# Expert stage in another order: the next expert's features and first products between this expert's steps, and the second 64 slots in one of two arms

## The chip, the cores and the metric

The kernel runs on one core of one Trainium2 chip. The metric is the device time of one execution in microseconds; the profile of one execution stands beside it. The engines are TensorE (PE), VectorE (DVE), ScalarE (ACT), GpSimd (POOL) and SyncE (SP, which only issues transfers here).

## What is computed

The kernel is a model of several stages, of which one appears twice here: a mixture of experts, after the mixing stage of each of two layers. Cut to what matters, the reference is:

```python
def hier_moe(h, w_rg, b_rg, w_re, b_re, w_gate, w_up, w_down):
    ...                                   # softmax scores, two experts of 32 for each token
    order = jnp.argsort(flat_e)           # token slots sorted by expert
    ...
    x_buf = h_pad[buf_tok].reshape(nblk, MOE_BLOCK, d)

    def run_block(args):
        xb, e = args
        return (jax.nn.silu(xb @ w_gate[e]) * (xb @ w_up[e])) @ w_down[e]

    y = lax.map(run_block, (x_buf, blk_e)).reshape(total, d)
    return jnp.zeros((n, d), h.dtype).at[tok_sorted].add(y[dest] * w_sorted[:, None].astype(h.dtype))
```

All is float32. A token has 1024 features; an expert has 512 hidden ones, so its gate, up and down matrices are 2 MB each.

## The kernel before

`moe` (L1035) runs the stage, once in each layer. Slots are dealt out so that each of the 32 experts (`NE`) has one block of 128 slots; tokens beyond that go to overflow blocks, which a loop at the end of `moe` runs with `expert`, one block a turn. The loop over the 32 experts in `experts` is unrolled. A block's 128 slots are two halves of 64. The first half always runs. The second runs only where the expert has more than 64 slots: `more` is read from the index table `tix` on every engine (L1286), and `tc.If(more < T)` (L1287) is a branch that each engine takes for itself.

For one expert the loop does the following.

- POOL gathers the rows of the expert after next into one of three buffers `xg` (`ex_load`, L1198).
- SP issues the next expert's weights: twelve tiles `wr` of 512 KB, four each of gate, up and down (`ex_load_w`, `wraw` at L105). They go through a ring of 32 tiles; a load into a tile waits until the products that read it are over. A down tile is 128 rows of 4 KB that lie 16 KB apart, one for each partition.
- `ex_in` (L1228): 16 first products on PE, eight slices of 128 features by gate and up. Gate goes to partitions 0 to 63 of one PSUM tile `ea`, up to the others. The profile counts each as two passes, 32 in all.
- `ex_act`: silu on ScalarE (L1234), then the product with the up half on VectorE (L1235), which writes `sg`.
- `ex_x` of the next expert: eight transposes of 64 rows of `xg` on PE (L1218), copied by VectorE to `xT` (L1220).
- `past[e]()`, in the experts 0 to 3: small steps that spread the gains, count the overflow and write its lists.
- `ex_at`: four transposes of `sg` on PE (L1241), copied by VectorE to `aT` (L1243).
- `ex_out` (L1252): eight second products (16 passes) into another PSUM tile `ea`; ScalarE scales them by the slot's weight in layer 0 (L1255), VectorE by weight and gain in layer 1 (L1257); POOL scatters `ey` to `Y` in DRAM (L1258).
- then the branch, and in its arm `ex_half`: the whole chain again for the other 64 slots, each step behind the one before.

PSUM tiles come from one pool of eight banks with the tag `b`; `xT`, `sg`, `aT` and `ey` have two buffers each. The order on each engine is set by a scheduler that places instructions as they become ready, within the order of the code on either side of a branch; `keep_in_program_order` pins an instruction against others that are pinned.

Of the kernel before, what the change touches and what calls it, by code (L numbers as in the profile page):

```python
# [8 lines left out]
F32 = mybir.dt.float32  # L9
# [4 lines left out]
AF = mybir.ActivationFunctionType  # L14
ALU = mybir.AluOpType
# [4 lines left out]
P = 128  # L20
# [5 lines left out]
NE = 32  # L26
# [16 lines left out]
class Ker:  # L43
# [1156 lines left out]

    def ex_w(self, name, l, e):
        w = self.I[name]
        w = w[l, e] if isinstance(e, int) else w[l, bass.ds(e, 1)].rearrange("o a b -> (o a) b")
        return w.rearrange("(p k) f -> p k f", p=P)

    def ex_load_w(self, l, e):

        gu = [self.ex_w(n, l, e) for n in ("moe_w_gate", "moe_w_up")]
        d = self.ex_w("moe_w_down", l, e)
        gu = [[self.wraw(w[:, k:k + 2, :]) for w in gu] for k in (0, 2, 4, 6)]  # L1210
        return gu, [self.wraw(d[:, k:k + 1, :]) for k in range(4)]

    def ex_x(self, xg, h, px, ps):

        r = slice(h * 64, h * 64 + 64)
        pt = ps.tile([P, 512], F32, name="pt", tag="b")
        for k in range(8):
            self.nc.tensor.transpose(pt[:, k * 64:k * 64 + 64], xg[r, k * P:(k + 1) * P], self.ident[r, r])  # L1218
        x = px.tile([P, 8, 64], F32, name="xT", tag="xT")
        self.nc.vector.tensor_copy(x, pt.rearrange("p (k t) -> p k t", k=8))  # L1220
        return x

    def ex_in(self, w, x, ps):

        a = ps.tile([P, 512], F32, name="ea", tag="b")
        for k in range(8):
            for j in range(2):
                self.nc.tensor.matmul(a[j * 64:j * 64 + 64, :], x[:, k, :], w[0][k // 2][j][:, k % 2, :], start=k == 0, stop=k == 7)  # L1228
        return a
# [8 lines left out]
    def ex_at(self, sg, px, ps):  # L1238
        pt = ps.tile([P, 512], F32, name="pt", tag="b")
        for k in range(4):  # L1240
            self.nc.tensor.transpose(pt[:, k * 64:k * 64 + 64], sg[64:, k * P:(k + 1) * P], self.ident[64:, 64:])  # L1241
        at = px.tile([P, 4, 64], F32, name="aT", tag="aT")
        self.nc.vector.tensor_copy(at, pt[:, :256].rearrange("p (k t) -> p k t", k=4))  # L1243
        return at

    def ex_out(self, w, at, idx, wl, Y, T, px, ps):

        nc = self.nc
        acc = ps.tile([P, 512], F32, name="ea", tag="b")
        for k in range(4):  # L1250
            for c in range(2):
                nc.tensor.matmul(acc[c * 64:c * 64 + 64, :], at[:, k, :], w[1][k][:, 0, c * 512:c * 512 + 512], start=k == 0, stop=k == 3)  # L1252
        y = px.tile([P, 512], F32, name="ey", tag="ey")
        if self.gain is None:
            nc.scalar.mul(y, acc, wl)  # L1255
        else:
            nc.vector.scalar_tensor_tensor(y, acc, wl, self.gain, ALU.mult, ALU.mult)  # L1257
        nc.gpsimd.indirect_dma_start(Y.rearrange("t (h d) -> (t h) d", h=2), bass.IndirectOffsetOnAxis(ap=idx, axis=0), y, None,  # L1258
                                     bounds_check=4 * T - 1, oob_is_err=False)

    def ex_half(self, w, h, xg, idx, wl, Y, T, px, ps):

        a = self.ex_in(w, self.ex_x(xg, h, px, ps), ps)
        self.ex_out(w, self.ex_at(self.ex_act(a, px), px, ps), idx[:, h], wl[:, h], Y, T, px, ps)

    def experts(self, l, tix, idx, wl, xg, hD, Y, T, px, ps, past, gains):

        nc = self.nc
        for e in range(2):
            self.ex_load(tix[:, e:e + 1], xg[e % 3], hD, T)  # L1270
        x = self.ex_x(xg[0], 0, px, ps)
        w = [self.ex_load_w(l, 0)]
        for e in range(NE):
            if e + 2 <= NE:
                self.ex_load(tix[:, e + 2:e + 3], xg[(e + 2) % 3], hD, T)
            if e + 1 < NE:
                w.append(self.ex_load_w(l, e + 1))
# [12 lines left out]
            if e == NE - 1:  # L1290
                gains()

    def expert(self, l, e, idx, wl, xg, Y, T, px, ps):
        w = self.ex_load_w(l, e)
        for h in range(2):
            self.ex_half(w, h, xg, idx, wl, Y, T, px, ps)


    def rpb_tables(self, pool):
# [865 lines left out]
```

## Time and profile before

| | us |
|---|---|
| three executions | 3675.94, 3684.01, 3686.07 |
| their median | 3684.01 |
| the profiled execution | 3679.17 |
| its span, first to last instruction | 3677.4 |
| PE busy | 3303.7 (90% of the span) |
| PE weight loads busy | 2146.6 (58%) |
| VectorE busy | 1483.9 (40%) |
| ScalarE busy | 1037.0 (28%) |
| GpSimd busy | 499.2 (14%) |

The profiled execution is one of its own, not one of the three. Busy times are a sum over stages with different limits, so a share of 90% doesn't say that PE sets the end of each stage; and a PE that is busy may run at either of two clock levels. `PEclk` in a row is the mean clock that was granted in its stretch, as a share of full speed (0.95 over the whole execution). In a row of the timeline, what stands in brackets is how long the engine was idle before the instruction and what it had waited for; `PEq`, `PEldq` or `SPq` is the sequencer of an engine, which handles branches, loads of registers and issues of transfers.

### The profile page before, as it was taken

How to read it: one execution, taken by the hardware profiler on the slowest of the kernel's cores; microseconds unless marked ns; L12 is line 12 of the kernel's file. 1: busy time of each engine (PE TensorE's matmuls, PEld its weight loads, DVE VectorE, ACT ScalarE, POOL GpSimd, SP SyncE). 2: the span in 40 equal slices, each digit the busy share in tenths (PEclk: the TensorE clock that was granted, in tenths of full speed). 3: DMA queues.
4: the chain of work that ended last, by engine and by line, in shares of the span. 5: the costliest groups of instructions: out<-in, count | busy, mean ns of one | idle time of the engine just before them, and what ended most of it. 6: DMA issues, size and time to landing. Idle time of an engine off the chain costs nothing.

```text
span 3677.4 us, 44411 instructions
## 1 busy us (share of the span) xinstructions
PE 3303.7 (90%) x16560; PEld 2146.6 (58%) x16560; DVE 1483.9 (40%) x2766; ACT 1037.0 (28%) x1809; POOL 499.2 (14%) x581
## 2 busy tenths in 40 slices
PE   7999988888888879998888887798999999999998
PEld 5954565332223378776333232676888877778887
DVE  3475664111111166666211111536543447355343
ACT  3465541111101134443000000325332324333232
POOL 1053511110011023331111110303000000000000
PEclk9999999898989889999999999899999999999999
DMA  5134456985799542226899995522323324233331
GB/s 197 49 132 150 150 182 241 384 344 191 273 362 393 211 143 78 66 60 237 328 407 394 398 396 203 187 81 73 112 93 97 92 44 101 81 93 103 92 92 46
DMA packets 351067, 676.15 MB, mean 184 GB/s; under 512 B 43028, under 2 KB 194772, under 8 KB 349408
## 3 DMA queue, kind: packets, MB, share of 16 engines
q1 hardware_dynamic: 313816, 626.50, 48.1%
q0 software_dynamic: 17584, 25.94, 2.0%
q10 hardware_dynamic: 19416, 20.34, 1.8%
q8 instruction: 160, 2.62, 0.3%
q14 instruction: 91, 0.75, 0.1%
HBM read 676.74 MB, written 29.45 MB: 192 GB/s over the span
## 4 chain that ended last, share of the span: by engine, by line
PE 34%; issue 10%; DMA 4%; DVE 2%; ACT 1%; POOL 0%; SPq 0%; POOLq 0%; ACTq 0%; DVEq 0%
PE aw L197 6%; PE aw L198 6%; PE aw L199 6%; PE acc L197 5%; PE acc L199 5%; PE acc L198 5%; DMA Y<-ey,idx 4%; PE s L1989 1%; PE o L1995 0%; ACT wh L116 0%; PE o L495 0%; PE pt L1725 0%; PE pt L299 0%; DMA yp<-Y 0%; DVE xO L1573 0%
## 5 line engine op out<-in xcount | busy, mean ns | idle before, releaser
L1228 PE MATMUL ea<-wr,xT 128*64 128x512 f32 x2368 | 544.0, 599 | 27.9 <-PEq L1287 13.6
L117 DVE TENSOR_TENSOR wh<-wr,wh 128x1024 fp32r<-128x1024 f32 (+2 forms) x276 | 339.2, 1235 | 319.5 <-ACT wh L116 319.0
L197 PE MATMUL aw<-hh,wh 128*128 128x512 f32 (+1 forms) x1216 | 446.7, 368 | 3.7 <-ACT wh L116 2.6
L198 PE MATMUL aw<-hl,wh 128*128 128x512 f32 (+1 forms) x1216 | 447.2, 368 | 1.6 <-DVE hl L193 1.6
L199 PE MATMUL aw<-hh,wh 128*128 128x512 f32 (+1 forms) x1216 | 446.0, 367 | 0.0
L116 ACT CAST wh<-wr 128x1024 fp32r<-128x1024 f32 (+2 forms) x276 | 281.0, 1026 | 448.8 <-PE acc L199 292.5
L1252 PE MATMUL ea<-wr,aT 128*64 128x512 f32 x1184 | 368.4, 780 | 42.2 <-DVE aT L1243 26.5
L1228 PEld LDWEIGHTS ea<-wr,xT 128*64 128x64 f32 x2368 | 190.3, 137 | 360.0 <-issue 272.8
L1220 DVE COPY xT<-pt 128x512 f32<-128x512 f32 x74 | 51.1, 691 | 660.0 <-PE pt L1218 660.0
L1234 ACT ACTIVATE sg<-ea 64x512 f32<-64x512 f32 x74 | 76.4, 1032 | 808.5 <-PE ea L1228 808.5
L197 PEld LDWEIGHTS aw<-hh,wh 128*128 128x128 f32 x1216 | 230.9, 190 | 45.6 <-ACT wh L116 3.5
L198 PEld LDWEIGHTS aw<-hl,wh 128*128 128x128 f32 x1216 | 231.0, 190 | 44.9 <-issue 3.5
L199 PEld LDWEIGHTS aw<-hh,wh 128*128 128x128 f32 x1216 | 230.8, 190 | 43.0 <-issue 3.5
L1252 PEld LDWEIGHTS ea<-wr,aT 128*64 128x64 f32 x1184 | 107.5, 175 | 245.5 <-issue 190.4
L467 POOL TENSOR_TENSOR pp<-pp,rc 128x768 f32<-128x768 f32 (+3 forms) x192 | 211.5, 1109 | 258.4 <-DVE rc L466 248.2
L1258 POOL DMA_INDIRECT Y<-ey,idx x74 | 74.8, 1011 | 961.8 <-DVEq L1287 355.0
L465 ACT ACTIVATE pp<-s,nm 128x768 f32<-128x768 f32 (+3 forms) x192 | 137.1, 716 | 156.6 <-DVE nm L1470 78.3
L197 PE MATMUL acc<-wh,hh 128*128 128x512 f32 (+2 forms) x480 | 177.4, 370 | 0.0
L198 PE MATMUL acc<-wh,hh 128*128 128x512 f32 (+2 forms) x480 | 176.3, 367 | 0.0
L199 PE MATMUL acc<-wh,hl 128*128 128x512 f32 (+2 forms) x480 | 175.9, 366 | 0.0
L1241 PE MATMUL pt<-c_ident,sg 64*128 64x64 f32 x296 | 34.7, 241 | 141.4 <-DVE sg L1235 141.3
L198 PE MATMUL acc<-wh,ah 128*128 128x512 f32 x352 | 139.5, 396 | 0.0
(479 smaller groups left out, 5101.5 us busy)
## 6 DMA issues: line engine op xcount, KB each, us to landing
wr<-in_moe_w_gate_dram SPq DMA_DIRECT2D x260, 512.0 KB
wr<-in_moe_w_up_dram SPq DMA_DIRECT2D x260, 512.0 KB
wr<-in_moe_w_down_dram SPq DMA_DIRECT2D x260, 512.0 KB
wr<-in_w_ada_dram SPq DMA_DIRECT2D x96, 512.0 KB
wr<-in_ffn_w_up_dram SPq DMA_DIRECT2D x88, 512.0 KB
wr<-in_ffn_w_down_dram SPq DMA_DIRECT2D x44, 512.0 KB
wr<-in_odd_w_in_dram SPq DMA_DIRECT2D x32, 512.0 KB
wr<-in_na_w_in_dram SPq DMA_DIRECT2D x30, 512.0 KB
```

The lines of the kernel that those rows point to most:

```text
L116: keep(self.nc.scalar.copy(hi, raw))
L117: keep((self.lo_eng or self.nc.vector).tensor_sub(lo, raw, f(hi)))
L197: mm(ps, ah, bh, start=first, stop=False)
L198: mm(ps, ah, bl, start=False, stop=False)
L199: mm(ps, al, bh, start=False, stop=last)
L465: nc.scalar.activation(p[:, :n], s[:, b:b + n], AF.Exp, bias=nm, scale=sign, accum_out=rc)
L467: nc.gpsimd.tensor_mul(p[:, :n], p[:, :n], rc.broadcast_to([P, n]))
L1220: self.nc.vector.tensor_copy(x, pt.rearrange("p (k t) -> p k t", k=8))
L1228: self.nc.tensor.matmul(a[j * 64:j * 64 + 64, :], x[:, k, :], w[0][k // 2][j][:, k % 2, :], start=k == 0, stop=k == 7)
L1234: self.nc.scalar.activation(by, a[:64].rearrange("t (p k) -> t p k", k=4), AF.Silu)
L1252: nc.tensor.matmul(acc[c * 64:c * 64 + 64, :], at[:, k, :], w[1][k][:, 0, c * 512:c * 512 + 512], start=k == 0, stop=k == 3)
L1258: nc.gpsimd.indirect_dma_start(Y.rearrange("t (h d) -> (t h) d", h=2), bass.IndirectOffsetOnAxis(ap=idx, axis=0), y, None, bounds_check=4 ...
```

## The change

The code's steps stay, in another order, and some in other pieces:

- The next expert's transposes (`ex_x`) and the first four products of it (`range(2)` of eight slices, by gate and up) are written between this expert's first products and its second ones. The first products come in three calls, for the slices 0 and 1, 2 to 4 and 5 to 7.
- `ex_x` transposes all 128 rows of a block at once, eight transposes of 128x128 in two PSUM tiles; ScalarE copies one half, VectorE the other. The second 64 slots read the same `xT`.
- `ex_act` works in two pieces of 256 columns in their own order. Before, the silu wrote its columns in an order with a stride of four.
- In line with that, a down tile is 128 consecutive rows of the matrix: 512 KB in one piece.
- This expert's second products go behind the branch, into both of its arms. The first arm, `ex_rest`, has the second half's first products, then the second products of the first half, then those of the second. The other arm has the second products of the first half alone.
- Products and transposes on PE are pinned to program order (`mmo`).

The diff, cut to its core:

```diff
-        return gu, [self.wraw(d[:, k:k + 1, :]) for k in range(4)]
+        return gu, [self.wraw(d[k * P:(k + 1) * P, :]) for k in range(4)]
...
+        x = px.tile([P, 8, P], F32, name="xT", tag="xT")
+        for g in range(2):
+            pt = ps.tile([P, 512], F32, name="pt", tag="b")
+            for k in range(4):
+                c = (g * 4 + k) * P
+                self.tc.keep_in_program_order(self.nc.tensor.transpose(pt[:, k * P:(k + 1) * P], xg[:, c:c + P], self.ident))
+            (self.nc.vector.tensor_copy if g else self.nc.scalar.copy)(x[:, g * 4:g * 4 + 4, :], pt.rearrange("p (k t) -> p k t", t=P))
         return x
...
-        by = self.by(sg[64:], 4)
-        self.nc.scalar.activation(by, a[:64].rearrange("t (p k) -> t p k", k=4), AF.Silu)
-        self.nc.vector.tensor_mul(by, by, a[64:].rearrange("t (p k) -> t p k", k=4))
+        for c in (slice(0, 256), slice(256, 512)):
+            self.nc.scalar.activation(sg[64:, c], a[:64, c], AF.Silu)
+            self.nc.vector.tensor_mul(sg[64:, c], sg[64:, c], a[64:, c])
...
+    def ex_rest(self, w, x, sg, out, px, ps):
+
+        a = ps.tile([P, 512], F32, name="ea", tag="b")
+        self.ex_in(a, w, x, 1, range(8))
+        sg2 = self.ex_act(a, px)
+        self.ex_out(w, sg, 0, *out)
+        self.ex_out(w, sg2, 1, *out)
...
-            a = self.ex_in(w[e], x, ps)
+                w1 = self.ex_load_w(l, e + 1)
+            self.ex_in(a, w, x, 0, range(2, 5))
+            if e + 1 < NE:
+                x1 = self.ex_x(xg[(e + 1) % 3], px, ps)
+            self.ex_in(a, w, x, 0, range(5, 8))
             sg = self.ex_act(a, px)
-            if e + 1 < NE:
-                x = self.ex_x(xg[(e + 1) % 3], 0, px, ps)
             if e < len(past):
                 past[e]()
-            at = self.ex_at(sg, px, ps)
-            self.ex_out(w[e], at, idx[:, 0, e:e + 1], wl[:, 0, e:e + 1], Y, T, px, ps)
+            if e + 1 < NE:
+                a = ps.tile([P, 512], F32, name="ea", tag="b")
+                self.ex_in(a, w1, x1, 0, range(2))
+            out = idx[:, :, e:e + 1], wl[:, :, e:e + 1], Y, T, px, ps
             more = nc.values_load(tix[64:65, e:e + 1], min_val=0, max_val=int(BIG))
-            with self.tc.If(more < T):
-                self.ex_half(w[e], 1, xg[e % 3], idx[:, :, e:e + 1], wl[:, :, e:e + 1], Y, T, px, ps)
-            w[e] = None
+            with self.tc.If(more < T) as many:
+                self.ex_rest(w, x, sg, out, px, ps)
+            with many.Else():
+                self.ex_out(w, sg, 0, *out)
+            w, x = w1, x1
```

Where the instructions stand is not the code's order alone, since products may be placed ahead of a branch up to the point that pins and buffers allow. Before, on PE, in an expert of layer 0 (`x16` is a count; `pt` is a PSUM tile of transposes, `ea` one of products, `c_ident` the identity matrix):

```order
L1228 MATMUL ea<-wr,xT 64x512 x16
L1218 MATMUL pt<-c_ident,xg_5784 128x64 x8
L1241 MATMUL pt<-c_ident,sg 128x64 x4
L1252 MATMUL ea<-wr,aT 64x512 x8
L1286 TENSOR_LOAD tix
L1287 COMPARE_AND_BRANCH
L1218 MATMUL pt<-c_ident,xg_5786 128x64 x8
L1228 MATMUL ea<-wr,xT 64x512 x16
L1241 MATMUL pt<-c_ident,sg 128x64 x4
L1252 MATMUL ea<-wr,aT 64x512 x8
L1287 UNCONDITIONAL_BRANCH x2
```

After, on PE at a like place of layer 0:

```order
L1246 MATMUL pt<-c_ident,sg 128x64 x4
L1213 MATMUL ea<-wr,aT 64x512 x8
L1294 UNCONDITIONAL_BRANCH
L1222 MATMUL pt<-c_ident,xg_5784 128x128 x8
L1213 MATMUL ea<-wr,xT 64x512 x10
L1293 TENSOR_LOAD tix
L1213 MATMUL ea<-wr,xT 64x512 x6
L1294 COMPARE_AND_BRANCH
L1213 MATMUL ea<-wr,xT 64x512 x16
L1246 MATMUL pt<-c_ident,sg 128x64 x4
L1213 MATMUL ea<-wr,aT 64x512 x8
L1246 MATMUL pt<-c_ident,sg 128x64 x4
```

The sixteen products between the transposes of `xg` and the branch are the last six of this expert and ten of the next. With the experts numbered from 0, ten stand there for each from 6 to 29 (one to seven for those before), and the transposes of `sg` have moved behind the branch. The same place in layer 1, in its experts 3 to 18:

```order
L1213 MATMUL ea<-wr,xT 64x512 x9
L1222 MATMUL pt<-c_ident,xg_15968 128x128 x8
L1213 MATMUL ea<-wr,xT 64x512 x7
L1293 TENSOR_LOAD tix
L1294 COMPARE_AND_BRANCH
```

Here only one of the seven products is the next expert's; nine of this expert's follow the last branch. From expert 19 of layer 1 on it is ten again. On VectorE in layer 0, before:

```order
L1220 COPY xT<-pt 128x512
L1235 TENSOR_TENSOR sg<-sg,ea 64x128x4
L1243 COPY aT<-pt 128x256
L1286 TENSOR_LOAD tix
L1287 COMPARE_AND_BRANCH
```

and after:

```order
L1223 COPY xT<-pt 128x512
L1236 TENSOR_TENSOR sg<-sg,ea 64x256 x2
L1293 TENSOR_LOAD tix
L1294 COMPARE_AND_BRANCH
L1247 COPY aT<-pt 128x256
L1236 TENSOR_TENSOR sg<-sg,ea 64x256 x2
L1247 COPY aT<-pt 128x256
L1294 UNCONDITIONAL_BRANCH
L1247 COPY aT<-pt 128x256
L1294 UNCONDITIONAL_BRANCH
```

The first arm now has the second half's product and both copies of `aT`, the second arm one copy. SP and POOL issue as many transfers as before, in the same order against each other.

## Rows read from the trace of the kernel before

**Rows 1.** tile `ey`: line, engine, xcount: ns min/median/max, first and last start us

```profile
L1255 ACT ACTIVATE ey<-ea,wl x40: 687/687/690, 628.4 to 1287.1; 128x512 f32<-128x512 f32 x40
L1257 DVE SCALAR_TENSOR_TENSOR ey<-ea,wl,gain x34: 750/751/752, 1761.5 to 2290.0; 128x512 f32<-128x512 f32 x34
```

**Rows 2.** busy us by stretch: PE, PEld, DVE, ACT, POOL; PEclk, DMA share, GB/s

```profile
762.00:967.00 205.00, 169.46 (x738) 59.45 (x735) 25.00 (x35) 20.62 (x24) 19.64 (x20) 0.88 0.66 246
...
967.00:1244.00 277.00, 227.55 (x987) 84.30 (x986) 35.70 (x50) 28.51 (x33) 31.57 (x31) 0.91 0.93 357
...
1836.00:2101.00 265.00, 217.07 (x1022) 81.74 (x1020) 49.14 (x68) 17.54 (x17) 34.70 (x34) 0.94 1.02 400
```

**Rows 3.** timeline, an expert of layer 1: start us, us, work, [idle before <-releaser]

```profile
2010.30 3.65 PE L1252 MATMUL ea<-wr,aT 128*64 128x512 f32 x16 [0.52 <-DVE aT L1243]
...
2014.26 7.09 PE L1228 MATMUL ea<-wr,xT 128*64 128x512 f32 x32 [0.31 <-PEq L1287]
...
2021.28 0.71 PE L1218 MATMUL pt<-c_ident,xg 64*128 64x64 f32 x8
...
2021.38 1.03 ACT L1234 ACTIVATE sg<-ea 64x512 f32<-64x512 f32 x1 [13.54 <-PE ea L1228]
...
2022.75 1.02 DVE L1235 TENSOR_TENSOR sg<-sg,ea 64x512 f32<-64x512 f32 x1
...
2023.91 0.43 PE L1241 MATMUL pt<-c_ident,sg 64*128 64x64 f32 x4 [1.93 <-DVE sg L1235]
...
2024.87 5.35 PE L1252 MATMUL ea<-wr,aT 128*64 128x512 f32 x16 [0.52 <-DVE aT L1243]
...
2030.53 7.09 PE L1228 MATMUL ea<-wr,xT 128*64 128x512 f32 x32 [0.31 <-PEq L1287]
```

**Rows 4.** waits, 1755 to 2293 us: who waits for whom: us, times, longest

```profile
PE pt L1241 <- DVE sg L1235: 62.5, 32, 2.4
...
PE ea L1252 <- DVE aT L1243: 19.0, 34, 1.7
```

**Rows 5.** timeline, SP's queue: first gate tiles of experts, last down tiles

```profile
1763.40 0.55 SPq L105 DMA_DIRECT2D wr<-in_moe_w_gate_dram  x1
...
2212.34 0.33 SPq L105 DMA_DIRECT2D wr<-in_moe_w_gate_dram  x1
...
2228.25 0.41 SPq L105 DMA_DIRECT2D wr<-in_moe_w_gate_dram  x1
...
2242.40 1.75 SPq L105 DMA_DIRECT2D wr<-in_moe_w_down_dram  x4
```

**Rows 6.** groups of instructions, L487: busy us, mean ns, idle before

```profile
L487 PE MATMUL pt<-c_ident,pp 128*128 128x128 f32 x448 | 69.0, 280 | 1.3 <-POOL pp L467 1.3
```

**Rows 7.** timeline, PE's weight loads in one expert

```profile
2019.43 0.17 PEld L1228 LDWEIGHTS ea<-wr,xT 128*64 128x64 f32 x2 [0.26 <-issue]
...
2021.28 0.57 PEld L1218 LDWEIGHTS pt<-c_ident,xg 64*128 64x128 f32 x8 [0.81 <-issue]
```

**Rows 8.** timeline, ScalarE in layer 0: `sg` of two neighbouring experts

```profile
831.79 1.03 ACT L1234 ACTIVATE sg<-ea 64x512 f32<-64x512 f32 x1 [6.13 <-PE ea L1228]
...
865.85 1.03 ACT L1234 ACTIVATE sg<-ea 64x512 f32<-64x512 f32 x1 [6.13 <-PE ea L1228]
```

**Rows 9.** timeline, ScalarE: the last expert of layer 0

```profile
1244.65 0.69 ACT L1255 ACTIVATE ey<-ea,wl 128x512 f32<-128x512 f32 x1 [7.54 <-PEq L1287]
```

**Rows 10.** waits of SP's DMA queue, 1755 to 2293 us

```profile
SPq L105 <- PEq L1287: 46.7, 15, 7.2
```

**Rows 11.** timeline, POOL in layer 1: a gather and a scatter

```profile
2016.68 1.02 POOL L1198 DMA_INDIRECT xg<-hD,tix  x1 [0.62 <-issue]
...
2229.32 1.00 POOL L1258 DMA_INDIRECT Y<-ey,idx  x1 [16.20 <-DVE ey L1257]
```

**Rows 12.** the line that issues the gathers, L1198

```profile
DMA to landing us min/median/max: 2.1/7.2/9.2
```

**Rows 13.** the branch's line, L1287, on PE: ns min/median/max

```profile
L1287 PEldq COMPARE_BRANCH  x72: 65/279/973, 625.3 to 2284.6; - x72
```

More of the change, by code (lines that the diff above doesn't have):

```diff
@@ L1202, in ex_w @@
         w = self.I[name]
-        w = w[l, e] if isinstance(e, int) else w[l, bass.ds(e, 1)].rearrange("o a b -> (o a) b")
-        return w.rearrange("(p k) f -> p k f", p=P)
+        return w[l, e] if isinstance(e, int) else w[l, bass.ds(e, 1)].rearrange("o a b -> (o a) b")
     def ex_load_w(self, l, e):
-        gu = [self.ex_w(n, l, e) for n in ("moe_w_gate", "moe_w_up")]
+        gu = [self.ex_w(n, l, e).rearrange("(p k) f -> p k f", p=P) for n in ("moe_w_gate", "moe_w_up")]
         d = self.ex_w("moe_w_down", l, e)
@@ L1210, in ex_load_w @@
         gu = [[self.wraw(w[:, k:k + 2, :]) for w in gu] for k in (0, 2, 4, 6)]
-        return gu, [self.wraw(d[:, k:k + 1, :]) for k in range(4)]
[L1213 to L1220, printed above, removed]
-        return x
@@ L1223, in ex_in, with mmo, ex_x @@
-    def ex_in(self, w, x, ps):
-        a = ps.tile([P, 512], F32, name="ea", tag="b")
-        for k in range(8):
+        return gu, [self.wraw(d[k * P:(k + 1) * P, :]) for k in range(4)]
+    def mmo(self, *a, **k):
+        self.tc.keep_in_program_order(self.nc.tensor.matmul(*a, **k))
+    def ex_x(self, xg, px, ps):
+        x = px.tile([P, 8, P], F32, name="xT", tag="xT")
[5 more added lines that the diff above has]
+            (self.nc.vector.tensor_copy if g else self.nc.scalar.copy)(x[:, g * 4:g * 4 + 4, :], pt.rearrange("p (k t) -> p k t", t=P))
+        return x
@@ L1227, in ex_in @@
+    def ex_in(self, a, w, x, h, ks):
+        for k in ks:
             for j in range(2):
-                self.nc.tensor.matmul(a[j * 64:j * 64 + 64, :], x[:, k, :], w[0][k // 2][j][:, k % 2, :], start=k == 0, stop=k == 7)
-        return a
+                self.mmo(a[j * 64:j * 64 + 64, :], x[:, k, h * 64:h * 64 + 64], w[0][k // 2][j][:, k % 2, :], start=k == 0, stop=k == 7)
     def ex_act(self, a, px):
         sg = px.tile([P, DE], F32, name="sg", tag="sg")
-        by = self.by(sg[64:], 4)
@@ L1234, in ex_act, with ex_out @@
-        self.nc.scalar.activation(by, a[:64].rearrange("t (p k) -> t p k", k=4), AF.Silu)
-        self.nc.vector.tensor_mul(by, by, a[64:].rearrange("t (p k) -> t p k", k=4))
-        return sg
-    def ex_at(self, sg, px, ps):
+        for c in (slice(0, 256), slice(256, 512)):
+            self.nc.scalar.activation(sg[64:, c], a[:64, c], AF.Silu)
+            self.nc.vector.tensor_mul(sg[64:, c], sg[64:, c], a[64:, c])
+        return sg
+    def ex_out(self, w, sg, h, idx, wl, Y, T, px, ps):
+        nc = self.nc
@@ L1239, in ex_at @@
         pt = ps.tile([P, 512], F32, name="pt", tag="b")
+        at = px.tile([P, 4, 64], F32, name="aT", tag="aT")
         for k in range(4):
[L1241 to L1248, printed above, removed]
+            self.tc.keep_in_program_order(
+                nc.tensor.transpose(pt[:, k * 64:k * 64 + 64], sg[64:, k * P:(k + 1) * P], self.ident[64:, 64:]))
@@ L1249, in ex_out @@
+        nc.vector.tensor_copy(at, pt[:, :256].rearrange("p (k t) -> p k t", k=4))
         acc = ps.tile([P, 512], F32, name="ea", tag="b")
@@ L1251, in ex_out @@
             for c in range(2):
-                nc.tensor.matmul(acc[c * 64:c * 64 + 64, :], at[:, k, :], w[1][k][:, 0, c * 512:c * 512 + 512], start=k == 0, stop=k == 3)
+                self.mmo(acc[c * 64:c * 64 + 64, :], at[:, k, :], w[1][k][:, c * 512:c * 512 + 512], start=k == 0, stop=k == 3)
         y = px.tile([P, 512], F32, name="ey", tag="ey")
         if self.gain is None:
-            nc.scalar.mul(y, acc, wl)
+            nc.scalar.mul(y, acc, wl[:, h])
         else:
-            nc.vector.scalar_tensor_tensor(y, acc, wl, self.gain, ALU.mult, ALU.mult)
-        nc.gpsimd.indirect_dma_start(Y.rearrange("t (h d) -> (t h) d", h=2), bass.IndirectOffsetOnAxis(ap=idx, axis=0), y, None,
+            nc.vector.scalar_tensor_tensor(y, acc, wl[:, h], self.gain, ALU.mult, ALU.mult)
+        nc.gpsimd.indirect_dma_start(Y.rearrange("t (h d) -> (t h) d", h=2), bass.IndirectOffsetOnAxis(ap=idx[:, h], axis=0), y, None,
                                      bounds_check=4 * T - 1, oob_is_err=False)
-    def ex_half(self, w, h, xg, idx, wl, Y, T, px, ps):
-        a = self.ex_in(w, self.ex_x(xg, h, px, ps), ps)
-        self.ex_out(w, self.ex_at(self.ex_act(a, px), px, ps), idx[:, h], wl[:, h], Y, T, px, ps)
+    def ex_rest(self, w, x, sg, out, px, ps):
[4 more added lines that the diff above has]
+        self.ex_out(w, sg2, 1, *out)
     def experts(self, l, tix, idx, wl, xg, hD, Y, T, px, ps, past, gains):
@@ L1270, in experts @@
             self.ex_load(tix[:, e:e + 1], xg[e % 3], hD, T)
-        x = self.ex_x(xg[0], 0, px, ps)
-        w = [self.ex_load_w(l, 0)]
+        x = self.ex_x(xg[0], px, ps)
+        w = self.ex_load_w(l, 0)
+        a = ps.tile([P, 512], F32, name="ea", tag="b")
+        self.ex_in(a, w, x, 0, range(2))
         for e in range(NE):
@@ L1276, in experts @@
             if e + 1 < NE:
-                w.append(self.ex_load_w(l, e + 1))
-            a = self.ex_in(w[e], x, ps)
+                w1 = self.ex_load_w(l, e + 1)
[3 more added lines that the diff above has]
+            self.ex_in(a, w, x, 0, range(5, 8))
             sg = self.ex_act(a, px)
-            if e + 1 < NE:
-                x = self.ex_x(xg[(e + 1) % 3], 0, px, ps)
             if e < len(past):
                 past[e]()
-            at = self.ex_at(sg, px, ps)
-            self.ex_out(w[e], at, idx[:, 0, e:e + 1], wl[:, 0, e:e + 1], Y, T, px, ps)
+            if e + 1 < NE:
+                a = ps.tile([P, 512], F32, name="ea", tag="b")
+                self.ex_in(a, w1, x1, 0, range(2))
+            out = idx[:, :, e:e + 1], wl[:, :, e:e + 1], Y, T, px, ps
             more = nc.values_load(tix[64:65, e:e + 1], min_val=0, max_val=int(BIG))
-            with self.tc.If(more < T):
-                self.ex_half(w[e], 1, xg[e % 3], idx[:, :, e:e + 1], wl[:, :, e:e + 1], Y, T, px, ps)
-            w[e] = None
+            with self.tc.If(more < T) as many:
[3 more added lines that the diff above has]
+            w, x = w1, x1
             if e == NE - 1:
@@ L1294, in expert @@
         w = self.ex_load_w(l, e)
-        for h in range(2):
-            self.ex_half(w, h, xg, idx, wl, Y, T, px, ps)
+        x = self.ex_x(xg, px, ps)
+        a = ps.tile([P, 512], F32, name="ea", tag="b")
+        self.ex_in(a, w, x, 0, range(8))
+        self.ex_rest(w, x, self.ex_act(a, px), (idx, wl, Y, T, px, ps), px, ps)
     def rpb_tables(self, pool):
```

## The prediction

> **What bounds the kernel now.** I read the engine table above first: TensorE (PE) is the busiest engine by far. The change touches only the two expert stages. The rows of `ey`, written once per half of 64 slots, give their extent [rows 1]: 40 halves in layer 0, from 628.4 to 1287.1 us, and 34 in layer 1, at 1761.5 to 2290.0 us. With 32 experts a layer and one overflow expert of two halves in layer 0, that makes six second halves in layer 0 and two in layer 1.
>
> Next the busy time by stretch [rows 2]. In layer 1, from 1836 us on, the DMA engines are full: share 1.02, 400 GB/s. In layer 0, from 762 to 967 us, where all six second halves lie, the share is 0.66 at 246 GB/s, and 0.93 behind them. So layer 1 has two limits close together, and layer 0 is mostly PE's.
>
> Last the timeline of one expert [rows 3]. Its first products run from 2014.26 for 7.09 us. Then PE does 0.71 and 0.43 us of transposes inside 3.59 us (2021.28 to 2024.87), because the sigmoid product takes ScalarE 1.03 and then VectorE 1.02 us, one behind the other. In this expert the second products took 5.35 us; one expert earlier they took 3.65 us, the same sixteen passes. [...] Start to start is 16.27 us here, and 14.57 us with the 3.65. The wait list of layer 1 says the same [rows 4]: 62.5 us in 32 waits for `sg`, then 19.0 us in 34 waits for `aT` (0.56 each).
>
> How fast can loads go? An expert needs twelve tiles of 512 KB. The first gate tiles of two neighbouring experts were issued at 2212.34 and 2228.25 [rows 5], with the DMA full: 15.91 us an expert, 1.326 a tile.
>
> **The change part by part.**
>
> *A single expert on PE.* The first products are as many as before: 7.09 us. The transposes of `xg` are now eight of 128x128 for both halves at once; the nearest row has 69.0 us for 448 such, 0.154 each [rows 6], so 1.23 us against 0.71. The transposes of `sg` stay, 0.43, and so does the wait for `aT`, 0.56. The second products take 3.65 us if the clock holds. A jump cost 0.31 us of PE idle time before [rows 3]; a single expert now takes one into the second arm and one out of it: 0.62. Two more changes between tile shapes come in, for which I put 0.5 in all. Sum: 14.1 us.
>
> The 1.9 us of idle time for `sg` goes, because up to ten products of the next expert stand there now: 20 of the 32 passes that took 7.09 us, so 4.4 us. The chain behind them is at most 1.03 + 1.02. For most experts of layer 1 the order puts only one product there, 0.4 us; up to 1.7 us of idle time stays: 15.8 us, still under the 15.91 of the loads.
>
> On the tile shapes the row shows first: the weight loads of the `xg` transposes start with a gap of 0.81 us, inside a run of products it is 0.26 [rows 7], 0.55 more; PE's own row of these transposes shows no idle time [rows 3]. The two ends are nothing and 2 x 0.55; my 0.5 lies between. [...]
>
> *An expert with a second half.* Before: the `sg` rows of such an expert and of the next lie at 831.79 and 865.85, so 34.06 us [rows 8]. After: 14.1 plus 7.09 of products, 0.43, 0.56 and 3.65, so 25.8 us. Its second chain lies beside the second products of the first half. I save 8.2 us, six times in layer 0.
>
> *Layer 0.* Before, the experts 1 to 31 took from 628.4 to about 1244 [rows 1, 9]: 616 us. After: 25 x 14.1 + 6 x 25.8 + 4 us (the overflow lists that fill the experts 1 to 3, which lay in the idle time; an estimate) = 511, so 1139. Do the loads follow? At the end of the second halves the ring of 32 tiles is full. The last 17 experts need 204 tiles, of which 20 to 32 are there: 172 to 184 x 1.326 = 228 to 244 us against 17 x 14.1 = 240. I add 8 us of waiting: 1147. The gains and the overflow expert took from 1244 to 1287, 43 us; there two chains go, 36 us. That is 1183 for 1287: 104 us, of which I count **102**.
>
> *Layer 1.* PE is at the pace of the loads already. SP was held by PE for 46.7 us in 15 waits [rows 10], but mostly with data still moving (DMA share 1.02). The issue at 1763.40 is the first tile of the fourth expert [rows 5], so 36 were out; the other 348 at 1.326 take 461 us, to 2225, where the last was issued at 2242 to 2244. So 0 to 18 us come from there; I take 9. The two second halves lie late, in the experts 28 and 31: one is scattered at 2229.32 after POOL's 16.20 us for its `ey` [rows 11], the other ends the stage at 2290.0 [rows 1]. That is 2 x 8.2, and about 3 from the two singles between. **28 us**.
>
> *Queues.* SP's loads and POOL's gathers and scatters keep their number and their place against each other. But PE now transposes the next rows right behind the branch, some 7 us earlier. A gather was issued at 2016.68 [rows 11], 2.7 us after the second products of the expert before had ended (2010.30 + 3.65 [rows 3]), and lands in 7.2 us, at most 9.2 [rows 12]. With 14.1 us between, it is hidden by 2 to 4 us; without that cover PE would wait for it in each expert. The down tiles are read from 512 KB in one piece instead of rows 16 KB apart. No row shows that; tiles of the other kind take 1.326 us, and I take the same, with 5% either way on a third of the bytes (0.3 us an expert). The silu in two pieces on VectorE and ScalarE costs nothing on the path where ten products cover it; without them it is the 1.7 above.
>
> Sum: 130 us. The profiled execution took 3679.2, so 3549; the median of before is 4.8 above it, so **3554 us**, with 3520 to 3580 as the range of this case.
>
> **Rivals.**
>
> *The clock falls as before.* PE still idles 0.56 + 0.31 around the `sg` transposes. If all second products stay at 5.35: 38 x 1.7 in layer 0 less the 8 of waiting is 57, in layer 1 only the last six count, 10: 3621. If half of them do, 3588. Against it: the 5.35 came behind 1.9 us of idle time that goes.
>
> *The loads are the slower bound.* If the full pace is 16.9 us an expert (down tiles slower, or the gathers in the way), layer 1 loses 29 us and the tail of layer 0 some 17: 3600. Against it: the 15.91 was measured with gathers in it.
>
> *The order does not do what the diff says.* If in layer 0 too only one product stood before the branch, 25 x 1.7 = 42: 3596. The order of layer 0 shown above speaks against it.
>
> *Jumps: slower.* PE's compare-and-branch took 279 ns in the median and 973 at most [rows 13], and PE lost 0.31 [rows 3]. If the jump over the longer first arm stalls the engine for s us an expert, layer 0 loses 32 s and layer 1 32 (s - 1.8). The gain of 130 is gone at s = 2.9; at 3.5 it is 112 + 54 - 130 = 36 slower, 3720. For it: the arm that is jumped over has some 1.5 times the instructions of the old one. Against it: the 72 jumps of before stay under 1 us. [...]
>
> **How the numbers follow.** Forecast 0.59; clock 0.17; loads 0.08; order 0.04; everything hidden that I priced, and PE at the floor (13.5 us an expert, under 3520) 0.03; small gains from several of these, down to 3673, 0.02; no difference 0.02; jumps 0.05. A measurement of this kernel can tell 0.3% (11 us) from no change. Faster 0.93, same 0.02, slower 0.05. The range of 8 in 10 takes the forecast, half of the clock case, the loads and the order: 3515 to 3605.
>
> **What would show it.** Right: the `sg` wait of PE nearly gone and the `aT` wait at 0.5 us; second products at 3.65 us; single experts of layer 0 at 14 to 15 us, with a second half at 25 to 26, and the last ones at 16; layer 0 over at about 1183; in layer 1 PE waiting for weight tiles, at 15.9 an expert. Wrong: second products of 5.35 us in most experts, transposes that wait for the gather, idle time of over 1 us behind a branch, or a load pace above 16.5 us.

## The result, and the profile after

The changed kernel takes 3571.57 us (median of four runs, 3566.61 to 3573.04) where the kernel before takes 3680.3 (median of four; the table ahead of the prediction has three of them): a ratio of 0.9701, 95% interval 0.9682 to 0.9720, or 109 us saved. The forecast was 3554, with 3515 to 3605. The profiled execution took 3571.68 us, its span is 3569.9.

The extent of the two expert stages, by the rows of `ey` (as [rows 1]: first and last start):

```profile
L1254 ACT ACTIVATE ey<-ea,wl x40: 687/687/690, 632.5 to 1195.3; 128x512 f32<-128x512 f32 x40
L1256 DVE SCALAR_TENSOR_TENSOR ey<-ea,wl,gain x34: 750/751/752, 1673.3 to 2181.6; 128x512 f32<-128x512 f32 x34
```

Layer 0 ends at 1195.3 instead of 1287.1, 92 us earlier. Layer 1 ends at 2181.6 instead of 2290.0, 108 us earlier, so 16.6 us are its own.

Busy time by stretch, as [rows 2] (PE, PEld, DVE, ACT, POOL; granted clock, DMA share, GB/s):

```profile
762.00:967.00 205.00, 194.26 (x947) 69.78 (x948) 29.70 (x63) 29.35 (x62) 28.33 (x28) 1.00 0.92 352
967.00:1150.00 183.00, 163.13 (x660) 52.64 (x656) 21.20 (x43) 21.05 (x44) 20.31 (x20) 1.00 1.02 399
1836.00:2101.00 265.00, 229.16 (x943) 76.57 (x940) 42.29 (x78) 21.37 (x48) 31.58 (x31) 0.95 1.02 395
```

The granted clock of layer 0 went from 0.88 and 0.91 to 1.00. Before, of 6800 stretches of 0.25 us from 600 to 2300 us, 5635 have 1.00 and 1049 have 0.50, the two levels: it is 1.00 over the second products of 3.65 us at 2010.30 [rows 3] and 0.68 over those of 5.35 us at 2024.87, with 0.50 from 2026 to 2028. The DMA engines, at 0.66 and 0.93 in layer 0 before, are now at 0.92 and then at 1.02.

A single expert of layer 0, in the timeline of PE and ScalarE (start, us, work, idle before):

```profile
925.23 3.65 PE L1213 MATMUL ea<-wr,aT 128*64 128x512 f32 x16 [0.57 <-DVE aT L1247]
...
928.82 1.09 PE L1222 MATMUL pt<-c_ident,xg 128*128 128x128 f32 x8
...
929.84 7.09 PE L1213 MATMUL ea<-wr,xT 128*64 128x512 f32 x32
...
932.68 0.38 ACT L1235 ACTIVATE sg<-ea 64x256 f32<-64x256 f32 x1 [2.45 <-PE ea L1213]
...
936.86 0.46 PE L1246 MATMUL pt<-c_ident,sg 64*128 64x64 f32 x4
...
937.89 3.65 PE L1213 MATMUL ea<-wr,aT 128*64 128x512 f32 x16 [0.57 <-DVE aT L1247]
```

From second products to second products it is 12.66 us. The 32 passes are the last twelve of this expert and twenty of the next; the silu starts after the twelve, and its chain is over long before PE comes to `sg` at 936.86. PE idles 0.57 us in the whole expert. An expert with a second half takes 24.03 us from one to the next:

```profile
871.32 3.65 PE L1213 MATMUL ea<-wr,aT 128*64 128x512 f32 x16 [0.52 <-DVE aT L1247]
...
895.35 3.65 PE L1213 MATMUL ea<-wr,aT 128*64 128x512 f32 x16 [0.52 <-DVE aT L1247]
```

So PE does even better than forecast (14.1 and 25.8). What holds it is the loads. Here are the first gate tiles of the fourth and of the last expert in layer 1, as in [rows 5]:

```profile
1670.74 0.46 SPq L105 DMA_DIRECT2D wr<-in_moe_w_gate_dram  x1
...
2134.08 0.33 SPq L105 DMA_DIRECT2D wr<-in_moe_w_gate_dram  x1
```

That is 463.3 us for 28 experts, 16.55 each. Between the like rows of before, 1763.40 and 2228.25 [rows 5], there are 464.9 us and 28 experts as well: 16.60 each. **Layer 1 moved at the pace of the loads before and moves at it now.** Before, some tiles stood ready and PE hardly waited for them; it was SP, in the stretch of [rows 4], that waited for landings, and far longer than for PE (46.7 us [rows 10]):

```profile
SPq L105 <- DMA wr<-in_moe_w_down_dram: 121.7, 114, 2.0
SPq L105 <- DMA wr<-in_moe_w_up_dram: 82.4, 87, 1.6
SPq L105 <- DMA wr<-in_moe_w_gate_dram: 82.3, 92, 2.0
...
PE ea L1228 <- DMA wr<-in_moe_w_gate_dram: 1.3, 4, 0.4
PE ea L1228 <- DMA wr<-in_moe_w_up_dram: 1.3, 2, 0.9
```

PE now waits for tiles where it waited for `sg` [rows 4] (after, 1665 to 2190 us):

```profile
PE ea L1213 <- DVE aT L1247: 18.5, 31, 0.9
PE ea L1213 <- DMA wr<-in_moe_w_gate_dram: 18.0, 11, 5.0
PE ea L1213 <- DMA wr<-in_moe_w_up_dram: 9.5, 14, 1.3
PE pt L1246 <- DVE sg L1236: 5.3, 17, 0.5
```

Where the 92 us of layer 0 come from shows in SP's queue: the first gate tile of the experts 11 and 18, before and then after (numbered from 0; the second halves lie in 8 and 10 to 14, and SP runs two to three experts ahead of PE).

```profile
767.20 0.33 SPq L105 DMA_DIRECT2D wr<-in_moe_w_gate_dram  x1
...
978.54 0.52 SPq L105 DMA_DIRECT2D wr<-in_moe_w_gate_dram  x1
```

```profile
767.77 0.33 SPq L105 DMA_DIRECT2D wr<-in_moe_w_gate_dram  x1
...
914.45 0.33 SPq L105 DMA_DIRECT2D wr<-in_moe_w_gate_dram  x1
```

Up to the tile of expert 11 nothing is gained. From there to that of expert 18 the loads come 64 us ahead; about 9 us follow up to that of expert 31, and 19 behind it. The same by the starts of `ey`, expert by expert: the six experts with second halves took 203.1 us and now take 148.2, which is 55 of the 92. The eight single experts among and ahead of them gave 7 us and the 17 behind them 21 (283.3 to 262.2). Gains and overflow expert gave 13, and the layer began 4 us later. With the 1.5 us of layer 1's stream, the single experts of both layers, 56 in all, gave some 30 us, though PE alone now needs up to 3.6 us less for one (16.27 to 12.66): much of that saving is hidden.

### The profile page after: what moved, and what is told of

Read it like the earlier page. It is cut to its first block, busy times and chain, and to the rows that moved or that the text cites. A ratio compares the mean times of both kernels' runs of the same rounds, so it can differ in the third digit from the quotient of the medians.

```text
span 3569.9 us, 44389 instructions
## 1 busy us (share of the span) xinstructions
PE 3301.0 (92%) x16488; PEld 2125.6 (60%) x16488; DVE 1465.3 (41%) x2831; ACT 1051.5 (29%) x1948; POOL 498.9 (14%) x581
## 5 line engine op out<-in xcount | busy, mean ns | idle before, releaser
L1213 PE MATMUL ea<-wr,xT 128*64 128x512 f32 x2368 | 625.3, 604 | 48.7 <-DMA wr<-in_moe_w_up_dram 25.6
L1213 PE MATMUL ea<-wr,aT 128*64 128x512 f32 x1184 | 280.4, 615 | 43.7 <-DVE aT L1247 39.0
L197 PEld LDWEIGHTS aw<-hh,wh 128*128 128x128 f32 x1216 | 230.6, 190 | 45.8 <-ACT wh L116 3.4
L1213 PEld LDWEIGHTS ea<-wr,aT 128*64 128x64 f32 x1184 | 82.9, 140 | 186.4 <-issue 128.8
L1247 DVE COPY aT<-pt 128x256 f32<-128x256 f32 x74 | 31.4, 424 | 332.4 <-PE pt L1246 332.4
L1223 ACT COPY xT<-pt 128x512 f32<-128x512 f32 x65 | 37.8, 582 | 389.3 <-PE pt L1222 386.1
L1235 ACT ACTIVATE sg<-ea 64x256 f32<-64x256 f32 x148 | 55.6, 375 | 300.6 <-PE ea L1213 248.6
```

Source lines behind the costliest of these rows:

```text
L197: mm(ps, ah, bh, start=first, stop=False)
L1213: self.tc.keep_in_program_order(self.nc.tensor.matmul(*a, **k))
L1223: (self.nc.vector.tensor_copy if g else self.nc.scalar.copy)(x[:, g * 4:g * 4 + 4, :], pt.rearrange("p (k t) -> p k t", t=P))
L1235: self.nc.scalar.activation(sg[64:, c], a[:64, c], AF.Silu)
```

## The experiments

Theory L: the loads, at 16.6 us an expert, set the end of single experts in both layers; PE's saving there is hidden, and the time came mostly from the experts with second halves. Rival P: the time came from PE's saving in each expert.

**1. No product of the next expert ahead of the branch**, the rest as changed:

```diff
-            if e + 1 < NE:
-                a = ps.tile([P, 512], F32, name="ea", tag="b")
-                self.ex_in(a, w1, x1, 0, range(2))
             out = idx[:, :, e:e + 1], wl[:, :, e:e + 1], Y, T, px, ps
...
+            if e + 1 < NE:
+                a = ps.tile([P, 512], F32, name="ea", tag="b")
+                self.ex_in(a, w1, x1, 0, range(2))
             w, x = w1, x1
```

> The changed kernel, but none of the next expert's first products stands ahead of the branch: all sixteen follow it, with the arms, the transposes and the tiles as changed. Theory L (the weight loads, 16.6 us an expert, set the end of most experts in both layers, and PE's 12.7 us an expert lies under them): PE waits for sg again, about 1.9 us, and many second products take 5.35 us again, so a single expert takes 15 to 16 us on PE, still under the loads; only the experts near each layer's end show it. 3575 to 3590 us. Rival P (the gain of the change is PE time per expert, 2.5 to 3.5 us in each of 56 single experts): 3650 us or more.

3559.28 us (3555.57 to 3563.98), ratio 0.9671 (0.9648 to 0.9694). The idle time is back, and in many experts the 5.35 us as well; here one of layer 1, in PE's timeline:

```profile
2001.67 0.30 PE L1246 MATMUL pt<-c_ident,sg 64*128 64x64 f32 x2 [1.03 <-DVE sg L1236]
...
2002.45 0.33 PE L1246 MATMUL pt<-c_ident,sg 64*128 64x64 f32 x2 [0.47 <-DVE sg L1236]
...
2003.35 5.35 PE L1213 MATMUL ea<-wr,aT 128*64 128x512 f32 x16 [0.57 <-DVE aT L1247]
```

Single experts take 14.4 or 16.1 us, and yet the kernel is not slower; it is 12 us faster than the changed one. P falls. L had expected a small loss; why there is a gain instead, run 9 takes up.

**2. One arm again**: second products ahead of the branch, the arm with the second half's chain alone, and next products ahead as before:

```diff
-            with self.tc.If(more < T) as many:
-                self.ex_rest(w, x, sg, out, px, ps)
-            with many.Else():
-                self.ex_out(w, sg, 0, *out)
+            self.ex_out(w, sg, 0, *out)
+            with self.tc.If(more < T):
+                self.ex_rest(w, x, out, px, ps)
```

(`ex_rest` then has the second half's products, its `ex_act` and its `ex_out`; the ten next products are written in one piece.)

> The changed kernel, but this expert's second products stand ahead of the branch again and the only arm has the second half's chain alone (next expert's products still ahead of the branch, ten of them). Theory L: a single expert stays at 12.7 us of PE, an expert with a second half goes from 24.0 to 26.5 to 28 us, because its sg chain lies bare again; six such in layer 0, where PE and not the loads is late, and two near the end of layer 1, so 12 to 30 us: 3585 to 3600 us. Rival: the arms bring nothing, the order ahead of the branch does it all: 3568 to 3576 us.

3608.9 us (3605.73 to 3610.25), ratio 0.9807 (0.9785 to 0.9829): 37 us slower than the changed kernel, more than L's 12 to 30. Layer 0 ends at 1217.2, 22 us later; SP's steps through the experts with second halves are 26.9 us (one 28.4), in the changed kernel 24.0. The run doesn't undo the arms alone: without a branch between, products of the next expert also got in among the second products in many experts.

**3. The down tiles' transfers in the old shape**, nothing else changed:

```diff
-        return gu, [self.wraw(d[k * P:(k + 1) * P, :]) for k in range(4)]
+        return gu, [self.wraw(d.rearrange("(p k) f -> p k f", p=P)[:, k, :]) for k in range(4)]
```

> The changed kernel with the down tiles' transfers in the old shape: rows 16 KB apart instead of 512 KB in one piece (the outputs are another permutation, so not the reference's; the work on all engines is the same). Theory L with the pace set by bytes: 16.6 us an expert either way, 3565 to 3578 us. Rival (the shape of the down transfers is part of the gain): a pace of 17 us or more, 3582 us or more.

3569.93 us (3568.56 to 3572.0): no difference. The layout of the down tiles is worth nothing by itself.

**4. The kernel before, with PE kept busy** between its transposes of `xg` and `sg`, by four products that nobody reads:

```diff
+        a = ps.tile([P, 512], F32, name="fp", tag="b")
+        for j in range(4):
+            self.nc.tensor.matmul(a[:64, :], x[:, 7, :], w[0][3][j % 2][:, 1, :], start=True, stop=True)
...
+            self.fill_pe(w[e], x0, ps)
             at = self.ex_at(sg, px, ps)
```

> The kernel before with four products of no use (1.8 us of PE work) between the transposes of xg and those of sg of each first half, where PE idled 1.9 us; nothing else is changed, so PE has more work and no more help. Clock theory (the second products took 5.35 us because the idle time ahead of them let the clock fall): nearly all second products of first halves take 3.65 us, a single expert 14.6 us instead of 14.6 to 17, and the time falls by 10 to 40 us as far as the loads let it: 3640 to 3670 us. Rival (the 5.35 us are due to something else, such as weight tiles that come late or traffic of the transfers): 5.35 us stays in most of them, and the time is 3680 us or more.

```profile
2003.96 3.65 PE L1235 MATMUL fp<-wr,xT 128*64 128x512 f32 x8
...
2007.54 0.46 PE L1247 MATMUL pt<-c_ident,sg 64*128 64x64 f32 x4
...
2008.52 3.65 PE L1258 MATMUL ea<-wr,aT 128*64 128x512 f32 x16 [0.52 <-DVE aT L1249]
```

The timeline of PE in layer 1 shows second products of 3.65 us behind the filler. They are so nearly everywhere: 36 stretches of 3.65 us in layer 0, where the kernel before has 10. The granted clock is 1.00 from 1800 to 2100 us, where the kernel before has 0.93 to 0.95. So the clock theory holds: idle time ahead of them had slowed the second products. But the filler took 3.65 us, not the 1.8 that I had put down, and an expert takes 16.2 us. The 10 to 40 us that I had expected did not come; the time is 3679.19 (3677.39 to 3691.49), ratio 1.0004 (0.9990 to 1.0019). The clock was given back and the filler ate it.

**5 and 6. Without the loads of the down tiles**, in the changed kernel and in the one before (the second products read gate tiles):

```diff
-        return gu, [self.wraw(d[k * P:(k + 1) * P, :]) for k in range(4)]
+        return gu, [g[0].rearrange("p k f -> p (k f)") for g in gu]
```

> The changed kernel without the loads of the down tiles: the second products read the expert's gate tiles instead, so eight tiles are loaded for an expert instead of twelve (the outputs are not the reference's; all other work is the same). Theory L: 8 tiles take 11.1 us at 1.383 a tile, less than PE's 12.7, so PE sets the pace: layer 0 ends 60 to 80 us earlier, layer 1 takes 50 to 70 us less: 3425 to 3465 us, single experts at 12.7 to 14.4 us. Rival P (PE or the waits between engines set the pace in the changed kernel): less than 30 us gained, 3540 us or more.

> The kernel before without the loads of the down tiles, as in the run beside it. Theory L: here PE's 14.6 to 17 us an expert lies close to the 16.6 of the loads or over them, so little is gained: 10 to 45 us, 3635 to 3670 us. With the run beside it the change is then worth 180 to 240 us, about twice the 109 measured: the other half is what the loads take. Rival P: both kernels gain alike, and the difference stays near 109 us.

3436.67 us for the changed one (3435.19 to 3438.15), ratio 0.9346 (0.9314 to 0.9379); 3654.86 for the one before (3648.61 to 3657.36), ratio 0.9946 (0.9915 to 0.9976). In layer 1, changed and then before (busy by stretch, and what SP waited for longest in it):

```profile
1800.00:1960.00 160.00, 149.56 (x718) 55.33 (x717) 32.59 (x60) 16.02 (x36) 23.54 (x24) 1.00 0.89 326
SPq L105 <- PE ea L1212: 87.6, 23, 12.1
```

```profile
1800.00:1960.00 160.00, 129.94 (x624) 49.52 (x622) 31.04 (x43) 11.35 (x11) 20.41 (x20) 0.95 0.79 291
SPq L105 <- PEq L1286: 109.9, 10, 12.0
```

In both the loads now wait for PE. The changed kernel gains 135 us; the one before gains 20, for its single experts of layer 1 go on taking 14.6 and 16.3 us in turn. The same change is then worth 218 us, twice the 109. **The missing half is under the loads.** This is the clearest of the runs.

**7. Gathers for the first three experts of a layer alone:**

```diff
-            if e + 2 <= NE:
+            if e == 0:
                 self.ex_load(tix[:, e + 2:e + 3], xg[(e + 2) % 3], hD, T)
```

> The changed kernel with gathers of xg for the first three experts of a layer alone; the others read rows that are there already (the outputs are not the reference's). In the trace of the changed kernel the queue of gathers and scatters holds 4.6% of the DMA engines' time in layer 1. If the loads' pace is the DMA engines' and shared by share of time, gathers being most of it: 16.0 us an expert instead of 16.6, and 20 to 40 us in all: 3530 to 3552 us. Rival (the pace is that of one queue, whatever the other does): 16.6 us stays, 3565 to 3576 us.

3535.72 us (3532.73 to 3538.7), ratio 0.9616 (0.9578 to 0.9653). The loads' pace in layer 1, by the same two tiles:

```profile
1652.41 0.50 SPq L105 DMA_DIRECT2D wr<-in_moe_w_gate_dram  x1
...
2093.85 0.33 SPq L105 DMA_DIRECT2D wr<-in_moe_w_gate_dram  x1
```

441.4 us for 28 experts: 15.77 instead of 16.55, and 36 us in all. The queue of gathers and scatters had 4.6% of the DMA engines' time in the changed kernel (1700 to 2100 us) and has 2.1% here (1700 to 2050 us); leaving out the gathers took 4.7% off the time of an expert's loads, more than the queue's share fell by. So the pace is not one queue's; the loads share it with the gathers. Whether the DMA engines or the memory behind them set it, the run doesn't tell.

The pace of the loads is also the same whatever the order on PE. Over these 28 experts it is 16.5 to 16.7 us in every kernel here with all its loads and gathers, but for run 11 (17.0).

**8 and 9. The changed kernel and run 1's kernel once more, side by side.**

> The changed kernel once more, as the measure for the two beside it: 3566 to 3576 us.

> The changed kernel with no product of the next expert ahead of the branch, once more. Where the loads set the pace, products of the next expert that stand ahead of this one's second products make PE wait for the next expert's tiles before it ends this one. By this theory 3554 to 3564 us, 8 to 16 us less than the changed kernel beside it; if the 12 us of the first comparison were chance, 3566 to 3576.

3570.61 us (3565.55 to 3571.84) and 3562.15 us (3560.95 to 3570.17); ratios 0.9698 (0.9671 to 0.9724) and 0.9683 (0.9656 to 0.9711). The difference is 8 us, after 12 the first time: on the same side twice, but near the limit of what can be told. In run 1, PE's waits for gate tiles in layer 1 are gone from among the first products, and those for up tiles are

```profile
PE ea L1213 <- DMA wr<-in_moe_w_up_dram: 1.3, 7, 0.2
```

against the 18.0 and 9.5 us above. Where the tiles come late, a next expert's product that stands ahead of this one's second products makes PE wait with work at hand. Within the stream that costs nothing (463 and 464 us for the 28 experts of layer 1 in the changed kernel and run 8, 465 and 466 in runs 1 and 9). The gain lies at the ends of the layers: from the last expert's first tile to the last `ey` it is 64.8 and 63.3 us in layer 0 with the products ahead, 61.1 and 57.8 without; in layer 1 twice 47.5 against 42.6 and 45.8.

**10. Next products ahead of the branch in the experts 29 and 30 alone** (run 1's kernel, with the lines of the changed one for these two):

```diff
+            if NE - 3 <= e < NE - 1:
+                a = ps.tile([P, 512], F32, name="ea", tag="b")
+                self.ex_in(a, w1, x1, 0, range(2))
```

> As the run before it, but in the experts 29 and 30 of each layer, behind which no loads are left to wait for, the next expert's products stand ahead of the branch. By the theory PE saves 1.7 to 3.4 us in each of these where it is late and not the loads: 3 to 9 us less than the run before it. If those experts too wait for the loads: no difference.

3567.73 us (3563.51 to 3569.49), ratio 0.9691 (0.9665 to 0.9717): no gain, rather 6 us more than run 9. These experts too wait for their loads. In layer 0, six products of expert 29 (twelve passes) are followed by ten of expert 30, the first of which waits for its tile with expert 29's second products still to do:

```profile
1118.71 2.79 PE L1213 MATMUL ea<-wr,xT 128*64 128x512 f32 x12
...
1124.16 7.38 PE L1213 MATMUL ea<-wr,xT 128*64 128x512 f32 x20 [2.66 <-DMA wr<-in_moe_w_gate_dram]
...
1132.50 3.65 PE L1213 MATMUL ea<-wr,aT 128*64 128x512 f32 x16 [0.57 <-DVE aT L1247]
```

The end of layer 0, 57.8 us in run 9, is 65.1 here, as in the changed kernel; that of layer 1 stays at 42.6. So in layer 0 the products of these two experts bring the loss back, which bears out the reason given; at 2 to 7 us a layer the sizes stay near the limit of what can be told.

**11. The arms alone, in the kernel before:**

```diff
-            at = self.ex_at(sg, px, ps)
-            self.ex_out(w[e], at, idx[:, 0, e:e + 1], wl[:, 0, e:e + 1], Y, T, px, ps)
...
+            with self.tc.If(more < T) as many:
+                a2 = self.ex_in(w[e], self.ex_x(xg[e % 3], 1, px, ps), ps)
+                sg2 = self.ex_act(a2, px)
+                self.ex_out(w[e], self.ex_at(sg, px, ps), *o0)
+                self.ex_out(w[e], self.ex_at(sg2, px, ps), *o1)
+            with many.Else():
+                self.ex_out(w[e], self.ex_at(sg, px, ps), *o0)
```

> The kernel before with one part of the change alone: the second products of the first half stand behind the branch, in both arms, and the second half's first products ahead of them in the first arm. Transposes of 64 rows, silu in one piece, down tiles in rows and no product of the next expert ahead of the branch. If the arms carry most of the gain (an expert with a second half at about 26 us instead of 34, and gate and up tiles free for loads as soon as the branch is taken, some 5 us earlier): 3565 to 3600 us. If the gain needs the other parts: 3630 us or more.

3671.76 us (3665.06 to 3681.16), ratio 0.9980 (0.9962 to 0.9997). My theory on the arms fell. They do what they should, 26 to 28 us for an expert with a second half instead of 34. But look at a single expert of layer 1, and at the clock of a stretch of layer 0:

```profile
2018.29 7.03 PE L1228 MATMUL ea<-wr,xT 128*64 128x512 f32 x32
...
2027.90 0.56 PE L1241 MATMUL pt<-c_ident,sg 64*128 64x64 f32 x4 [1.93 <-DVE sg L1235]
...
2029.03 6.54 PE L1252 MATMUL ea<-wr,aT 128*64 128x512 f32 x16 [0.57 <-DVE aT L1243]
...
2035.40 7.03 PE L1228 MATMUL ea<-wr,xT 128*64 128x512 f32 x32
```

```profile
920.00:1150.00 230.00, 197.47 (x822) 68.26 (x820) 27.82 (x39) 23.03 (x27) 29.18 (x29) 0.81 0.99 378
```

Behind the second halves of layer 0 the second products of single experts now take 6.3 to 6.4 us, in most of layer 1 from 5.0 to 6.6, where before 3.65 and 5.35 took turns. Nearly every single expert there takes 17.1 us, more than the loads. By `ey` the arms save 40 us up to expert 14 of layer 0; 6.5 of them are lost again in the single experts behind and 14 in layer 1. The granted clock is 0.81. The idle time is as it was (1.93 and 0.57); what is gone is the 0.31 at the branch. Why the clock falls for longer with so little changed, the runs don't tell.

**12. Neither arms nor next products ahead**, so of the change only the transposes of 128 rows, the silu in two pieces and the down tiles:

> The changed kernel without both: no product of the next expert ahead of the branch, this expert's second products ahead of it, and one arm with the second half's chain alone. What is left of the change is the transposes of 128 rows, the silu in two pieces and the down tiles in one piece. If arms and early release carry the gain: an expert with a second half at 29 to 31 us, tiles released only behind the second products, 3620 to 3660 us. If the small parts carry it: 3590 us or less.

3639.23 us (3636.28 to 3643.07), ratio 0.9885 (0.9868 to 0.9901); its edit is that of run 1 and that of run 2 together. An expert with a second half takes 27.6 us. Layer 0 ends at 1244.1, 43 us earlier than before, and layer 1 takes as long as before (1003 us), so all of the gain is layer 0's. A single expert still shows the wait at the branch:

```profile
1998.82 4.51 PE L1213 MATMUL ea<-wr,xT 128*64 128x512 f32 x20 [0.31 <-PEq L1290]
```

Side by side, in us:

| | one arm | two arms |
|---|---|---|
| transposes, silu and down tiles as before | 3680 (before) | 3672 (run 11) |
| these three as changed | 3639 (run 12) | 3559, 3562 (runs 1, 9) |
| and next products ahead of the branch | 3609 (run 2) | 3572, 3571 (the change, run 8) |

The parts don't add up. The arms are worth 8 us on the old steps and 78 on the new ones. With the arms on the old steps a single expert takes 17.1 us (run 11), over the 16.6 of the loads; on the new ones, where the chain for `sg` is shorter (two pieces of 0.38 and 0.42 us, one behind the other, instead of 1.03 and 1.02), it takes 14.4 or 16.1 (runs 1 and 9). That this is why the arms' saving lasts there and not in run 11 is argued: no run held run 11's clock up. The next products ahead are worth 30 us with one arm, where they cover a bare chain, and less than nothing with two. Which of transposes and silu carries run 12's 42 us was not tried apart; the down tiles don't (run 3).

## Why the prediction was right, and where it was off

The time lies in the range, at 109 us of the 126 to 130 forecast (3554 lies 126 below the 3680.3 and 130 below the 3684.01 that it was worked out from). Point by point:

- **What bounds it.** Right: layer 1 at the pace of the loads, layer 0 PE's in the experts with second halves.
- **A single expert**, 14.1 us: PE takes 12.66. The 0.62 for jumps and the 0.5 for tile shapes are zero: the rows above show no idle time of PE there, and in the whole expert 0.57 us, ahead of the second products. In layer 1, where one product stands ahead, 15.8 had been put; while the tiles lasted it was 14.4, with 0.64 us of the wait for `sg` left. The clock held: 38 stretches of second products at 3.65 us in layer 0, 10 before, and a granted clock of 1.00 from 762 to 1150 us.
- **An expert with a second half**, 25.8 us: 24.0, and 28.2 for the first of the six. They were to save 49 us and by `ey` saved 55. The eight single experts up to there took 123.0 us where 117 had been put, with the lists. So the sum up to expert 14, 271.6 forecast and 271.2 measured, is right partly by luck: two misses cancel.
- **The pace of the loads**, 1.326 us a tile: this is the step that failed. I took it from one pair of experts, the last, whose 15.91 us is among the shortest steps of that stretch. Over the 28 steps between two rows that I had shown [rows 5] it is 16.60, 1.383 a tile. The sum even had the sign of it: 348 tiles at 1.326 ended at 2225, and the last tile was issued at 2242. I put these 18 us down to SP's waits for PE and booked half as a gain. They were the pace itself: layer 1's stream took 463.3 us instead of 464.9, a gain of 1.5 and not 9. The 16.55 is also just above the 16.5 that the prediction itself had named as a sign of being wrong.
- **The tail of layer 0.** The 17 single experts behind the second halves took 262 us (903.6 to 1165.9, by `ey`), not the 240 and 8 of waiting. The pace makes 10 of the 14; the other 4 no run takes apart. At 903.6 SP had issued 31 of these experts' tiles; how many had landed is not traced. Gains and overflow expert took 29 us, not 36, and the layer began 4 us later.
- **The end of layer 1**: from the last expert's first tile to the last `ey` 47.5 us, before 61.7: 14 us of the 19.
- **Queues.** PE waited for a gather once in each layer, ahead of its first expert: 2.9 and 1.2 us (before: 2.5 and 1.4). The down tiles' shape is worth nothing, as put (run 3: 3569.93 us against 3571.57).

| term | forecast | measured |
|---|---|---|
| layer 0 | 102 | 92 |
| layer 1, stream | 9 | 1.5 |
| layer 1, end | 19 | 14 |

The remaining 1 us lies at the start of layer 1.

The rivals: "the loads are the slower bound" had the right mechanism; its 16.9 was 16.55, and that was no slower than before. "The clock falls as before" did not happen to the second products here (3.65 us; over 1836 to 2101 us as a whole the granted clock is 0.95, 0.94 before). Run 1, where 29 of the 74 stretches of second products are slow again, shows no loss of time from it: its price of 34 to 67 us left out that the loads lie above. "The order" did not happen: the row of layer 0 above has twenty passes of the next expert ahead of the branch. "Jumps" did not happen; the branch's line on PE, as [rows 13]:

```profile
L1294 PEldq COMPARE_BRANCH  x72: 65/322/441, 624.5 to 2178.0; - x72
```

Not one of the rivals had what runs 1, 9 and 10 point to: that work pulled ahead can wait for its data in front of work that is ready.

## What to carry to other kernels

Take the pace of a saturated stream from the longest stretch that is full, first issue to last issue over the count, not from one step; and where a sum then misses a time in the trace, the miss is a term, not a gain. When two limits lie within a few per cent of each other, take one away in an experiment (here a third of the loads) before pricing the other: it showed a change worth 218 us of which 109 could be had. And order work by when its data come: products pulled ahead of ready ones helped an engine that waits for a chain (30 us here, runs 12 and 2), and cost 8 to 12 us where it waits for loads.

## What the hardware showed beyond that

- Four products into one half of a PSUM tile, eight passes, took 3.65 us (run 4), as long as eight products, sixteen passes, that go to its two halves in turn.
- The branch cost PE 0.31 us of idle time where it stands right behind the second products [rows 3] (and in run 12), and none in the changed kernel and in run 11, whose lists of PE's waits in the two stages have no line for `PEq`.
- Leaving out the gathers took 4.7% off the time of an expert's loads (16.55 to 15.77 us); their queue, scatters included, had had 4.6% of the DMA engines' time, and 2.1% is left (run 7).
- The same sixteen passes took 3.65, 5.35 or 6.54 us. The granted clock was 1.00 over the 3.65 and 0.68 over the 5.35 of [rows 3], and 0.81 over a stretch in which those of all single experts took 6.3 to 6.4 (run 11, 920 to 1150 us). With work in the place of the idle time ahead of them nearly all took 3.65 (run 4).
